# Operand steps one block ahead and W_out's parts on GpSimd's queue, in a hybrid encoder block

## The chip, the cores and the metric

The kernel runs on one core of one Trainium2 chip. The metric is the device time of one execution in microseconds. It is stated as the median of several runs; a profiled execution, taken separately, gives the trace that the views below are read from.

## What is computed

One layer on 1024 rows (tokens) of 1024 features in fp32: a SwiGLU feed-forward, a mixer (eight forgetting-attention heads beside an RG-LRU channel group) and a second feed-forward, each with a scaled residual and a layer norm:

```python
def layer_norm(x, g, b):
    mu = jnp.mean(x, axis=-1, keepdims=True)
    var = jnp.mean(jnp.square(x - mu), axis=-1, keepdims=True)
    return (x - mu) * lax.rsqrt(var + LN_EPS) * g + b

def swiglu(x, w_gate, w_up, w_down):
    return (jax.nn.silu(x @ w_gate) * (x @ w_up)) @ w_down

x = layer_norm(DN_ALPHA * x + 0.5 * swiglu(x, ffn1...), ln1_g, ln1_b)
z = x @ w_in                       # q, k, v, LRU inputs and gates, forget gates
fox = forgetting_attention(q, k, v, fg)     # softmax(q.k/8 + cum[t] - cum[s]) v, causal
lru = jax.nn.gelu(z_gate) * rg_lru(causal_conv(z_x))
x = layer_norm(DN_ALPHA * x + concat([fox, lru]) @ w_out, ln2_g, ln2_b)
x = layer_norm(DN_ALPHA * x + 0.5 * swiglu(x, ffn2...), ln3_g, ln3_b)
```

`D_MODEL` is 1024, `D_FF` 4096, the attention has 8 heads of 64 features, `cum` is the running sum of log forget gates.

## The kernel before

**Splitting.** TensorE multiplies fp32r operands. To keep fp32 accuracy each operand is split in two: ScalarE casts the high part, VectorE subtracts it from the source for the low part, and `mm3` (L159) sums three products, high by high, high by low and low by high. So nearly all the time of the kernel is 128x512 matmuls in threes, and each operand costs one ScalarE and one VectorE instruction ahead of them.

**Feed-forward.** `gate_up` (L334) computes x·W_gate and x·W_up for 16 pairs of 128 columns. Each product of a pair is done by a 2x2 block scheme with seven block products (`one` to `seven`, L650 to L672) whose operands are sums and differences of blocks, named "11", "t1", "22", "t2", "21", "t4", "t3" on the weights' side. In each pair `weights` (L361) loads 1 MB of W_gate and of W_up (SyncE's queue, L364; two buffers) and makes the seven split operands of each in a ring of 16 `ws` buffers. The first pair of the first feed-forward, `first_pair` (L376), has its ScalarE, VectorE and TensorE order written by hand, because it runs while x and the first weights still arrive. `down_ffn` (L740) is the third matrix.

**Steps done on the side.** The second feed-forward's first pair must start right behind the attention. Its seven operands of both matrices are therefore prepared during the first feed-forward by a generator, `prepare` (L263): a step loads a 128x256 block of the second W_gate or W_up into one of two `aux` buffers (L272), splits it (ScalarE L278, VectorE L279, in one buffer of the same `ws` ring), takes differences in place (L290, L296, L302, L307) and stores the two parts to a scratch tensor `pre_d` by GpSimd's queue (L285). Sixteen later steps do the same, without differences, for the attention half of W_out, into `wo_d` (L316, L317). `gate_up` calls for one step behind products `two` and `five` of each matrix of each pair from pair 1 on (L728), four in a pair; a step ends at a `yield`.

**Attention.** `attention` (L1122) goes through 64 units, one of 128 queries of one head each, heads 0 to 5 in turn from the longest unit to the shortest, then heads 6 and 7 interleaved. A unit's scores are computed by TensorE (L1158, L1159); GpSimd masks the diagonal block of `cum` in place (L1162); VectorE forms the logits from scores and `cum` with their extremum (L1164, which reads what the mask of the next shorter unit will write); ScalarE takes the exponentials (L1165). Three units later the probabilities are transposed (L1179), split (L1183, L1184) and multiplied with the values (L1200). A head's operands q, k (two parts), cum and v are loaded by SyncE's queue when the previous head reaches its third unit (`load`, L1132), two heads' buffers in all. Until unit 35, tiles of the W_out product for the LRU half fill TensorE (L1263). The attention half needs `wo_d`'s four pairs of parts (`ready_out_w`, L1114: SyncE's queue, one pair each at units 45, 47, 49, 51), in the eight `ws` buffers that the LRU half's parts had, and three of four pairs of `mix` blocks, the heads' outputs, which go out to DRAM by GpSimd's queue (L1216) and come back by SyncE's at units 40, 50, 52 (L1269). Behind the third of these stand norm 2's g and b, each broadcast to all partitions (`load_gb`, L188). They take the same eight `h` buffers, in order of asking. Output tiles with their norm (`layer_norm`, L195) follow from the last units on.

**Norm.** `layer_norm` subtracts the mean and multiplies by g (L205), then finds 1/sqrt(var + eps) from ScalarE's square root, a reciprocal and a Newton step (L206 to L210), and multiplies and adds b (L212). The Newton step here yields the negated factor, and `load_gb` negates g once by GpSimd (L192) to undo it.

**What sets the order.** A planner orders each engine's instructions at build time, by their place in the text and by when its model of the times holds them ready; on each engine, and on each engine's DMA queue, that order is then fixed, and an instruction that waits holds up what is behind it. `issue_after(x)` puts the instructions of its block that are on x's engine behind x. `fetch` (L99) keeps such a chain among SyncE's loads. `ready_pair` (L546) loads the prepared operands for the second feed-forward by SyncE's queue (L556).

Of the kernel before, what the change touches and what calls it, by code (L numbers as in the profile page):

```python
# [9 lines left out]
F32 = mybir.dt.float32  # L10
# [7 lines left out]
P = 128  # L18
# [41 lines left out]
class Block:  # L60
# [127 lines left out]
    def load_gb(self, g, b, gb):  # L188

        for t, v in zip(gb, (g, b)):  # L190
            self.fetch(t, bass.AP(tensor=v.tensor, offset=v.offset, ap=[[0, P], [1, D]]))
        self.nc.gpsimd.tensor_scalar(gb[0], gb[0], -1.0, 1.0, op0=ALU.mult, op1=ALU.mult)  # L192
        self.gb = gb

    def layer_norm(self, i, done=None):  # L195

        nc, v, gb = self.nc, self.nc.vector, self.gb
        a = self.acc[i]
        st = self.small.tile([P, 2, 6], F32, tag="st", name=self.nm("st"))
        for j in range(2):  # L200
            v.bn_stats(st[:, j, :], a[:, j * H:(j + 1) * H])
        s = self.small.tile([P, 8], F32, tag="ln", name=self.nm("ln"))
        mv, sd, y, w = s[:, 0:2], s[:, 2:3], s[:, 3:4], s[:, 4:5]
        v.bn_aggr(mv, st)
        v.scalar_tensor_tensor(a, a, mv[:, 0:1], gb[0], op0=ALU.subtract, op1=ALU.mult)  # L205
        nc.scalar.activation(sd, mv[:, 1:2], AF.Sqrt, bias=self.eps)  # L206
        v.tensor_scalar(w, mv[:, 1:2], EPS, 0.5, op0=ALU.add, op1=ALU.mult)
        v.reciprocal(y, sd)
        v.scalar_tensor_tensor(w, y, w, y, op0=ALU.mult, op1=ALU.mult)
        v.scalar_tensor_tensor(y, w, 1.5, y, op0=ALU.subtract, op1=ALU.mult)  # L210
        for ds in (slice(0, H), slice(H, D)) if done else (slice(0, D),):
            v.scalar_tensor_tensor(a[:, ds], a[:, ds], y, gb[1][:, ds], op0=ALU.mult, op1=ALU.add)  # L212
            if done:
                done(i, ds)
# [48 lines left out]
    def prepare(self, views, to_d, w_out, wsp, ap):  # L263

        nc, v = self.nc, self.nc.vector

        def raw():
            return ap.tile([P, 2, P], F32, tag="aux", name=self.nm("aux"))

        def load(view, k, c):  # L270
            t = raw()
            nc.sync.dma_start(t, view[:, k:k + 2, c * P:(c + 1) * P])  # L272
            return t

        def halves(src):
            t = wsp.tile([P, 4, P], F32R, tag="ws", name=self.nm("ws"))
            hi, lo = t[:, 0:2, :], t[:, 2:4, :]
            nc.scalar.copy(hi, src)  # L278
            v.tensor_tensor(lo, src, f32(hi), ALU.subtract)  # L279
            return t  # L280

        for m, view in enumerate(views):
            for h in range(2):
                def out(n, src):
                    nc.gpsimd.dma_start(to_d[m, OPERANDS.index(n), h], f32(halves(src)))  # L285

                up, down = 2 * h, 4 + 2 * h
                a, b = load(view, up, 0), load(view, up, 1)
                out("11", a)
                v.tensor_tensor(b, b, a, ALU.subtract)  # L290
                a = load(view, down, 1)
                yield
                out("t1", b)
                yield
                out("22", a)
                v.tensor_tensor(a, a, b, ALU.subtract)  # L296
                b = load(view, down, 0)
                yield
                out("t2", a)
                yield  # L300
                out("21", b)
                v.tensor_tensor(b, b, a, ALU.subtract)  # L302
                a = load(view, down, 1)
                yield
                out("t4", b)
                b = load(view, up, 1)
                v.tensor_tensor(a, a, b, ALU.subtract)  # L307
                yield
                out("t3", a)
                yield  # L310
        self.wo_d = self.dram.tile([FOX // P, P, 2, D], F32, name="wo_d")
        for f in range(FOX // P):
            for c in range(4):
                cols = slice(c * 2 * P, (c + 1) * 2 * P)
                a = raw()
                nc.sync.dma_start(a.rearrange("p k c -> p (k c)"), w_out[f * P:(f + 1) * P, cols])  # L316
                nc.gpsimd.dma_start(self.wo_d[f, :, :, cols], f32(halves(a)).rearrange("p (l k) c -> p l (k c)", l=2))  # L317
                yield

    def gu_views(self, *ws):  # L320
        return [w.rearrange("(k p) f -> p k f", p=P) for w in ws]
# [12 lines left out]
    def gate_up(self, wg, wu, h_d, rows, bank, tp, wsp, raws=None, later=None, aside=None, ready=None, steps=None):  # L334
# [26 lines left out]
        def weights(pair, view, w):  # L361

            r = self.raw([P, KT, 2 * P])
            nc.sync.dma_start(r, view[:, :, pair * 2 * P:(pair + 1) * 2 * P])  # L364
            b11, b12, b21, b22 = quarters(r)
            w["11"] = parts(b11)
            w["21"] = parts(b21)
            t1 = less(b12, b11)
            t2 = less(b22, t1)
            w["t2"] = parts(t2)  # L370
            w["t1"] = parts(t1)
            w["t3"] = parts(less(b22, b12))
            w["22"] = parts(b22)
            w["t4"] = parts(less(b21, t2))
# [171 lines left out]
        def ready_pair(g, u):  # L546
# [10 lines left out]
                                      ready[both.index(m), OPERANDS.index(n)].rearrange("h p (l k) f -> l p h k f", l=2)[l])  # L557
                m.w[n] = to

            for n in ("11", "21", "t1"):  # L560
                for m in both:
                    fetch(n, m, two_blocks())
            for n in ("t4", "t2"):
                r = self.rawp.tile([P, 4, 4, P], F32R, tag="raw", name=self.nm("raw"))
                for i, m in enumerate(both):
                    fetch(n, m, (r[:, 2 * i], r[:, 2 * i + 1]))
            t21 = [block() for _ in range(4)]
            g.sum, u.sum = self.sum_bank(), self.sum_bank()
            g.product("11", "11", g.sum, True)
# [112 lines left out]
        for pair in range(FF // P // 2):  # L682
# [39 lines left out]
            for m in (gate, up):  # L722
# [3 lines left out]
                for step in ("two", "six", "five", "seven", "three"):  # L726
                    getattr(m, step)()
                    if steps and step in ("two", "five"):  # L728
                        next(steps, None)

                def pending(m=m, gate=gate, g=(g0, g1), end=end, last=pair == FF // P // 2 - 1):
                    m.four()
# [381 lines left out]
    def ready_out_w(self):  # L1114

        for f in range(FOX // P):
            hl = tuple(self.wsp.tile([P, 4 * VW], F32R, tag="ws", name=self.nm("w"))[:, 0:D] for _ in range(2))
            for l in range(2):
                self.nc.sync.dma_start(f32(hl[l]), self.wo_d[f, :, l])
            yield hl  # L1120

    def attention(self, w_out, mixp, ln, normed):  # L1122
# [7 lines left out]
        with self.pool("att_p", 3) as pp, self.pool("att_t", 1) as tp, self.pool("att_pt", 6) as ptp, self.pool("att_qk", 2, side="right") as qkp:  # L1130
# [110 lines left out]
            for n in range(len(units) + AHEAD + 1):  # L1241
# [18 lines left out]
                if fill and (n < 2 or n % 8 in (2, 3, 4)):  # L1260
                    i, d = fill.pop(0)
                    with self.tc.issue_after(scores.ins) if n < 3 else nullcontext():
                        self.down_tile(i, lru_tiles, 1.0, (d,))  # L1263
                if 45 <= n < 53 and n % 2:
                    w_fox.append(next(w_steps))
                if n in MIXES:
                    mix.append(tuple(self.hp.tile([P, T], F32R, tag="h", name=self.nm("mix")) for _ in range(2)))
                    for l in range(2):
                        nc.sync.dma_start(f32(mix[-1][l]), mix_d[len(mix) - 1][l])  # L1269
                    if len(mix) == 3:  # L1270
                        self.load_gb(*ln, [self.hp.tile([P, T], F32, tag="h", name=self.nm("gb")) for _ in range(2)])
                if tiles:
                    out_tile()
            return tiles, out_tile
# [140 lines left out]
```

## Time and profile before

| | us |
|---|---|
| runs: median of 3 (lowest, highest) | 2322.07 (2321.42, 2322.68) |
| profiled execution: time | 2323.19 |
| its span, first to last instruction | 2321.5 |
| TensorE busy with matmuls | 2298.7 |
| VectorE busy | 1635.6 |
| ScalarE busy | 1019.1 |
| GpSimd busy | 227.8 |

The mean granted TensorE clock is 0.997. How to read the lines in the next sections: a row of a timeline is the start, the duration, engine, line, operation, written and read tile, and in brackets the idle time of the engine just before and what ended it; a row of waits is the waiting engine and line, what it waited for, total us, times and the longest; SPq and POOLq are the DMA issues of SyncE's and GpSimd's queues. Matmuls are pipelined: a 128x512 one is listed with 0.39 us while the next starts 0.23 us behind it.

### The profile page before, as it was taken

The page shows a single profiled execution, that of the slowest core. Times are in us where ns is not written, and L with a number is a line of the kernel's source. Part 1 is how long each engine was busy: PE and PEld are TensorE (multiplying, and loading weights), DVE is VectorE, ACT ScalarE, POOL GpSimd, SP SyncE. Part 2 cuts the span into 40 slices and gives each one's busy share as a digit, 9 for nine tenths or more (in the row PEclk, how much of TensorE's full clock was granted, in tenths as well). Part 3 has the DMA queues.
Part 4 walks back from the last instruction along what each step waited for, and adds up shares of the span by engine and source line. Part 5 has one row for each costly group of instructions (what it writes and reads, how often), then busy time and mean ns, then how long its engine had stood idle before and what let it go on. Part 6 is the DMA issues. An engine that isn't in the chain of part 4 may idle for free.

```text
span 2321.5 us, 28560 instructions
## 1 busy us (share of the span) xinstructions
PE 2298.7 (99%) x10705; PEld 1914.1 (82%) x10705; DVE 1635.6 (70%) x2521; ACT 1019.1 (44%) x1623; POOL 227.8 (10%) x388
## 2 busy tenths in 40 slices
PE   8999999999999999999999999999999999999998
PEld 7888888888888888888898788888888888888887
DVE  7867666666467788866667899565656665577886
ACT  5443434343344345453556755334333333344341
POOL 0121111100000000111133210000000000000000
PEclk9999999999999999999999999999999999999999
DMA  4444444433276433233274934232323232564542
GB/s 150 141 141 145 139 147 141 146 113 125 101 259 234 147 127 109 75 92 110 91 218 126 283 137 141 86 118 89 122 93 123 87 118 87 195 244 168 182 144 73
DMA packets 194444, 323.08 MB, mean 139 GB/s; under 512 B 10033, under 2 KB 115825, under 8 KB 194305
## 3 DMA queue, kind: packets, MB, share of 16 engines
q1 hardware_dynamic: 167712, 230.74, 30.9%
q0 software_dynamic: 26592, 90.51, 9.9%
q8 instruction: 84, 1.38, 0.3%
q14 instruction: 56, 0.45, 0.1%
HBM read 226.81 MB, written 94.40 MB: 138 GB/s over the span
## 4 chain that ended last, share of the span: by engine, by line
PE 81%; issue 10%; DVE 3%; DMA 3%; POOL 2%; ACT 1%; SPq 0%; POOLq 0%; DVEq 0%; ACTq 0%
PE x L163 7%; PE x L164 7%; PE x L165 7%; PE s L165 6%; PE s L164 6%; PE s L163 6%; PE a L165 6%; PE a L164 6%; PE a L163 6%; PE b L163 6%; PE b L164 6%; PE b L165 6%; PE a L1200 1%; PE a L1179 1%; PE a L1049 1%
## 5 line engine op out<-in xcount | busy, mean ns | idle before, releaser
L349 ACT CAST ws<-t 128x512 fp32r<-128x512 f32 x240 | 148.9, 623 | 374.2 <-PE b L164 253.0
L349 ACT CAST ws<-raw 128x512 fp32r<-128x512 f32 x180 | 111.0, 622 | 239.3 <-PE x L164 237.3
L350 DVE TENSOR_TENSOR ws<-t,ws 128x512 fp32r<-128x512 f32 x240 | 164.3, 686 | 56.4 <-ACT ws L349 50.6
L350 DVE TENSOR_TENSOR ws<-raw,ws 128x512 fp32r<-128x512 f32 x180 | 123.3, 688 | 114.4 <-ACT ws L349 110.3
L164 PE MATMUL a<-ws,ws 128*128 128x512 f32 x512 | 199.8, 390 | 0.2
L163 PE MATMUL a<-ws,ws 128*128 128x512 f32 x512 | 199.3, 390 | 0.4 <-ACT row L672 0.4
L163 PE MATMUL b<-As,ws 128*128 128x512 f32 x512 | 199.4, 389 | 0.2 <-ACT row L663 0.2
L164 PE MATMUL b<-As,ws 128*128 128x512 f32 x512 | 199.3, 389 | 0.0
L165 PE MATMUL b<-As,ws 128*128 128x512 f32 x512 | 199.2, 389 | 0.0
L165 PE MATMUL a<-ws,ws 128*128 128x512 f32 x512 | 199.2, 389 | 0.0
L163 PE MATMUL x<-As,ws 128*128 128x512 f32 x504 | 196.6, 390 | 2.1 <-ACT row L659 2.0
L164 PE MATMUL x<-As,ws 128*128 128x512 f32 x504 | 196.1, 389 | 0.0
L165 PE MATMUL x<-As,ws 128*128 128x512 f32 x504 | 196.1, 389 | 0.0
L163 PE MATMUL x<-A,ws 128*128 128x512 f32 x496 | 193.3, 390 | 0.0
L165 PE MATMUL x<-A,ws 128*128 128x512 f32 x496 | 193.0, 389 | 0.0
L164 PE MATMUL x<-A,ws 128*128 128x512 f32 x496 | 193.0, 389 | 0.0
L772 ACT CAST ws<-raw 128x1024 fp32r<-128x1024 f32 x112 | 117.4, 1050 | 157.8 <-PE a L164 87.2
L775 DVE TENSOR_TENSOR ws<-raw,ws 128x1024 fp32r<-128x1024 f32 x112 | 136.6, 1220 | 53.0 <-ACT ws L772 52.6
L702 POOL DMA_DIRECT2D h_d<-row x96 | 68.9, 719 | 968.5 <-DVE row L696 928.4
L163 PE MATMUL s<-ws,ws 128*128 128x512 f32 x384 | 149.5, 389 | 0.0
L165 PE MATMUL s<-ws,ws 128*128 128x512 f32 x384 | 149.4, 389 | 0.0
L164 PE MATMUL s<-ws,ws 128*128 128x512 f32 x384 | 149.4, 389 | 0.0
(295 smaller groups left out, 5252.7 us busy)
## 6 DMA issues: line engine op xcount, KB each, us to landing
raw<-h_d SPq DMA_DIRECT2D x56, 1024.0 KB, 5.4
h_d<-row POOLq DMA_DIRECT2D x96, 512.0 KB, 3.5
wd<-in_ffn_w_down_dram SPq DMA_DIRECT2D x32, 1024.0 KB, 7.5
raw<-in_ffn_w_gate_dram SPq DMA_DIRECT2D x30, 1024.0 KB, 5.3
raw<-in_ffn_w_up_dram SPq DMA_DIRECT2D x30, 1024.0 KB, 5.3
h_d<-row POOLq DMA_DIRECT2D x32, 256.0 KB, 2.7
raw<-in_w_in_dram SPq DMA_DIRECT2D x16, 512.0 KB, 4.9
pre_d<-ws POOLq DMA_DIRECT2D x28, 256.0 KB, 2.7
```

What stands on the lines that cost most here:

```text
L163: mm(out, ah, bh, start=first, stop=False, skip_group_check=goes_on)
L164: mm(out, ah, bl, start=False, stop=False, skip_group_check=goes_on)
L165: mm(out, al, bh, start=False, stop=last, skip_group_check=goes_on)
L349: nc.scalar.copy(hi, src)
L350: v.tensor_tensor(lo, src, f32(hi), ALU.subtract)
L702: nc.gpsimd.dma_start(d[:, 2 * n:2 * n + 2], t.rearrange("p (r t) -> p r t", r=2))
L772: cast = nc.scalar.copy(hi, src)
L775: self.mark = v.tensor_tensor(lo, src, f32(hi), ALU.subtract)
L1049: nc.tensor.matmul(pa[:, 0:width], xh, wh[:, 0:width], start=k == 0, stop=False)
L1179: nc.tensor.transpose(pa[:, (j % 4) * P:(j % 4 + 1) * P], p[:, j * P:(j + 1) * P], self.ident)
L1200: mm(pv[:, ps], vt[:, j, :], pts[h, qt][j // 4][l][:, j % 4, ps], start=j == 0 and l == 0, stop=j == last and l == 1)
```

## The change

Four things. In `prepare`, each block is loaded one step ahead of the step that uses it, so the order within the steps is shifted by one `yield`; W_out's steps too. 45 steps result where there were 44. In `gate_up`, the steps' SyncE instructions are put behind the pair's load of W_up. In the attention, W_out's parts are loaded by GpSimd's queue, at units 37, 39, 41 and 43, norm 2's vectors at unit 38 instead of with the third mix block at 52, and `ready_pair`'s first loads are put behind the last mix load. In the norms, g stays as it is, and the Newton step gives the factor with its own sign.

```diff
         for t, v in zip(gb, (g, b)):
             self.fetch(t, bass.AP(tensor=v.tensor, offset=v.offset, ap=[[0, P], [1, D]]))
-        self.nc.gpsimd.tensor_scalar(gb[0], gb[0], -1.0, 1.0, op0=ALU.mult, op1=ALU.mult)
...
-        v.tensor_scalar(w, mv[:, 1:2], EPS, 0.5, op0=ALU.add, op1=ALU.mult)
+        v.tensor_scalar(w, mv[:, 1:2], EPS, -0.5, op0=ALU.add, op1=ALU.mult)
...
-        v.scalar_tensor_tensor(y, w, 1.5, y, op0=ALU.subtract, op1=ALU.mult)
+        v.scalar_tensor_tensor(y, w, 1.5, y, op0=ALU.add, op1=ALU.mult)
...
                 up, down = 2 * h, 4 + 2 * h
                 a, b = load(view, up, 0), load(view, up, 1)
-                out("11", a)
-                v.tensor_tensor(b, b, a, ALU.subtract)
+                yield
+                keep(m, h, "11", a)
+                less(b, a)
                 a = load(view, down, 1)
                 yield
-                out("t1", b)
+                keep(m, h, "t1", b)
                 yield
-                out("22", a)
-                v.tensor_tensor(a, a, b, ALU.subtract)
+                keep(m, h, "22", a)
+                less(a, b)
                 b = load(view, down, 0)
...
-                out("t4", b)
+                keep(m, h, "t4", b)
                 b = load(view, up, 1)
-                v.tensor_tensor(a, a, b, ALU.subtract)
                 yield
-                out("t3", a)
-                yield
+                less(a, b)
+                keep(m, h, "t3", a)
...
                 nc.sync.dma_start(a.rearrange("p k c -> p (k c)"), w_out[f * P:(f + 1) * P, cols])
+                yield
                 nc.gpsimd.dma_start(self.wo_d[f, :, :, cols], f32(halves(a)).rearrange("p (l k) c -> p l (k c)", l=2))
-                yield
...
-            nc.sync.dma_start(r, view[:, :, pair * 2 * P:(pair + 1) * 2 * P])
+            self.weight_load = nc.sync.dma_start(r, view[:, :, pair * 2 * P:(pair + 1) * 2 * P])
...
+            with self.tc.issue_after(self.mix_load.ins):
+                for n in ("11", "21", "t1"):
+                    for m in both:
+                        fetch(n, m, two_blocks())
...
                     if steps and step in ("two", "five"):
-                        next(steps, None)
+                        with self.tc.issue_after(self.weight_load.ins):
+                            next(steps, None)
...
-                self.nc.sync.dma_start(f32(hl[l]), self.wo_d[f, :, l])
+                self.nc.gpsimd.dma_start(f32(hl[l]), self.wo_d[f, :, l])
...
-                if 45 <= n < 53 and n % 2:
+                if 36 <= n < 44 and n % 2:
                     w_fox.append(next(w_steps))
+                if n == 38:
+                    self.load_gb(*ln, [self.hp.tile([P, T], F32, tag="h", name=self.nm("gb")) for _ in range(2)])
                 if n in MIXES:
...
-                        nc.sync.dma_start(f32(mix[-1][l]), mix_d[len(mix) - 1][l])
-                    if len(mix) == 3:
-                        self.load_gb(*ln, [self.hp.tile([P, T], F32, tag="h", name=self.nm("gb")) for _ in range(2)])
+                        self.mix_load = nc.sync.dma_start(f32(mix[-1][l]), mix_d[len(mix) - 1][l])
```

More of the change, by code (lines that the diff above doesn't have):

```diff
@@ L280, in halves, with keep, less @@
             return t
+        def keep(m, h, n, src):
+            nc.gpsimd.dma_start(to_d[m, OPERANDS.index(n), h], f32(halves(src)))
+        def less(x, y):
+            v.tensor_tensor(x, x, y, ALU.subtract)
+        self.wo_d = self.dram.tile([FOX // P, P, 2, D], F32, name="wo_d")
         for m, view in enumerate(views):
             for h in range(2):
-                def out(n, src):
-                    nc.gpsimd.dma_start(to_d[m, OPERANDS.index(n), h], f32(halves(src)))
                 up, down = 2 * h, 4 + 2 * h
                 a, b = load(view, up, 0), load(view, up, 1)
-                out("11", a)
-                v.tensor_tensor(b, b, a, ALU.subtract)
+                yield
+                keep(m, h, "11", a)
+                less(b, a)
                 a = load(view, down, 1)
                 yield
-                out("t1", b)
+                keep(m, h, "t1", b)
                 yield
-                out("22", a)
-                v.tensor_tensor(a, a, b, ALU.subtract)
+                keep(m, h, "22", a)
+                less(a, b)
                 b = load(view, down, 0)
                 yield
-                out("t2", a)
+                keep(m, h, "t2", a)
                 yield
-                out("21", b)
-                v.tensor_tensor(b, b, a, ALU.subtract)
+                keep(m, h, "21", b)
+                less(b, a)
                 a = load(view, down, 1)
                 yield
-                out("t4", b)
+                keep(m, h, "t4", b)
                 b = load(view, up, 1)
-                v.tensor_tensor(a, a, b, ALU.subtract)
                 yield
-                out("t3", a)
-                yield
-        self.wo_d = self.dram.tile([FOX // P, P, 2, D], F32, name="wo_d")
+                less(a, b)
+                keep(m, h, "t3", a)
         for f in range(FOX // P):
@@ L558, in fetch @@
                 m.w[n] = to
[L560 to L566, printed above, removed]
+            with self.tc.issue_after(self.mix_load.ins):
+                for n in ("11", "21", "t1"):
+                    for m in both:
+                        fetch(n, m, two_blocks())
+                for n in ("t4", "t2"):
+                    r = self.rawp.tile([P, 4, 4, P], F32R, tag="raw", name=self.nm("raw"))
+                    for i, m in enumerate(both):
+                        fetch(n, m, (r[:, 2 * i], r[:, 2 * i + 1]))
             t21 = [block() for _ in range(4)]
```

## The prediction

> **What bounds the kernel now.** I read the page first, then TensorE's waits, then the chain of waits and the timelines at the few places where TensorE waits at all.
>
> ```profile
> span 2321.5 us, 28560 instructions
> PE 2298.7 (99%) x10705; PEld 1914.1 (82%) x10705; DVE 1635.6 (70%) x2521; ACT 1019.1 (44%) x1623; POOL 227.8 (10%) x388
> PE b L163 <- ACT ws L443: 2.8, 1, 2.8
> PE s L1158 <- DVE m L1164: 2.4, 7, 0.9
> PE x L163 <- ACT row L659: 2.0, 3, 1.2
> PE a L165 <- DMA mix<-mix_d: 0.2, 1, 0.2
> ```
>
> TensorE is busy for 2298.7 of 2321.5 us, and the change touches none of its 10705 matmuls. What can be won is therefore idle time, 22.8 us in all, and the part near the edits is the four rows above (total, times, longest), 7.4 us. 0.2% of the time, about what a measurement of this kernel can tell from no change, is 4.6 us. What can be lost is not bounded in this way: any new wait of TensorE counts in full.
>
> **The change, part by part.**
>
> *The prepared steps.* In the kernel before, the first step loads two blocks and at once subtracts them (L290) ahead of its first yield. The planner put that subtraction far ahead of its place in the text. Chain of waits and the engines' timelines, first 51 us (start, duration, and in brackets the idle time before and what ended it):
>
> ```profile
> 11.03 8.45 DMA aux<-in_ffn_w_gate_dram
> 17.73 3.66 PE L249 MATMUL b<-ident,x 128*128 128x128 f32 x32
> 50.30 0.39 SPq L364 DMA_DIRECT2D raw<-in_ffn_w_up_dram  x1
> 15.62 1.29 DVE L391 TENSOR_TENSOR ws<-raw,ws 128x512 fp32r<-128x512 f32 x2
> 19.57 0.43 DVE L290 TENSOR_TENSOR aux<-aux,aux 128x256 f32<-128x256 f32 x1 [2.66 <-DMA aux<-in_ffn_w_gate_dram]
> 19.91 0.68 DVE L391 TENSOR_TENSOR ws<-t,ws 128x512 fp32r<-128x512 f32 x1
> 23.56 0.58 ACT L443 COPY ws<-b 128x512 f32<-128x512 f32 x1
> 24.19 0.50 PE L163 MATMUL b<-A,ws 128*128 128x512 f32 x1 [2.80 <-ACT ws L443]
> ```
>
> VectorE finished at 15.62 + 1.29 = 16.91 and then stood 2.66 us before an operation that belongs to the second feed-forward layer, because that one's block landed as the last of the start-up loads. What first_pair needed next (L391) began at 19.91 instead of 16.91: 3.0 us late. ScalarE's copy at 23.56 comes behind it, and with it TensorE's 2.80 us. After the change the subtraction stands behind a yield, and the two loads are issued behind pair 1's load of w_up, which in the old trace goes out at 50.30 us; the subtraction cannot start before that. So the 3.0 us on VectorE go. What is late next? The transposes feeding that copy end at 17.73 + 3.66 = 21.39, so TensorE can go on there instead of at 24.19: 2.8 us.
>
> The stall has a second part. Stretches of 1 us: length, busy of TensorE, weight load, VectorE, ScalarE and GpSimd, granted clock, DMA share, GB/s:
>
> ```profile
> 25.00:26.00 1.00, 1.00 (x5) 0.84 (x4) 1.00 (x2) 0.66 (x2) 0.00 (x0) 0.80 0.00 0
> 26.00:27.00 1.00, 1.00 (x4) 0.72 (x4) 0.91 (x3) 0.79 (x2) 0.00 (x0) 0.50 0.00 0
> 27.00:28.00 1.00, 1.00 (x4) 0.81 (x3) 1.00 (x2) 1.00 (x3) 0.00 (x0) 0.50 0.00 0
> 28.00:29.00 1.00, 1.00 (x4) 0.81 (x3) 0.65 (x2) 0.78 (x2) 0.00 (x0) 0.50 0.00 0
> ```
>
> The granted clock fell to 0.50 for about 3.4 us right behind the wait (0.80 is 0.4 us at half clock, then 3 us whole). Half of 3.4 is 1.7 us of matmul time lost, and I expect no such dip when the wait is gone. The Trainium skill, "TensorE: Matmul & The Clock Gate", Part 1, states that the clock halves after at least one idle window of about 3.4 us. Here 2.8 us of idling did it, so the measurement goes by a looser rule than the page's; strictly by the page the dip would have another cause, and could stay, which leaves 2.8 us instead of 4.5.
>
> Together 4.5 us at most. But VectorE sets a second limit later in the same pair:
>
> ```profile
> 28.51 0.69 DVE L436 TENSOR_TENSOR row<-b,row 128x512 f32<-128x512 f32 x1 [0.35 <-PE b L165]
> 31.56 0.69 DVE L436 TENSOR_TENSOR row<-b,row 128x512 f32<-128x512 f32 x1 [0.56 <-PE b L165]
> 56.97 0.68 DVE L391 TENSOR_TENSOR As<-ws,As 128x512 fp32r<-128x512 f32 x1
> 57.71 0.50 PE L164 MATMUL b<-As,ws 128*128 128x512 f32 x1
> ```
>
> The matmul at 57.71 reads the low part that VectorE ended at 57.65: no slack there. TensorE can be ahead at that point only by what VectorE is ahead: 3.0 us, plus what its own waits for TensorE give back (0.35 and 0.56, 0.9 in all). I take **3.6 us** between 3.0 and 3.9 (2.8 and 4.5 as outer bounds).
>
> In the other pairs the steps run in bunches behind the pair's splits. Where ScalarE stood before a DMA, TensorE's three L659 waits came right after:
>
> ```profile
> 168.17 0.41 ACT L278 CAST ws<-aux 128x256 fp32r<-128x256 f32 x1 [0.70 <-DMA aux<-in_ffn_w_gate_dram]
> 398.87 0.62 ACT L349 CAST ws<-t 128x512 fp32r<-128x512 f32 x1 [2.19 <-DMA wo_d<-ws]
> 437.83 0.62 ACT L349 CAST ws<-t 128x512 fp32r<-128x512 f32 x1 [2.38 <-DMA wo_d<-ws]
> ```
>
> The first waited for a block; this is what loading a step ahead removes. The other two waited for a split buffer still being stored to W_out's scratch, and the change leaves these stores, two to four of them in a bunch, as they are. The number of casts and subtractions is unchanged (the subtractions move a step; one more step is needed, 45 for 44). Of the 2.0 us in the row of waits I take **0.8 us** as gained. It can be 2.0 (all three go) or a loss: with the phase shifted by one step another bunch may be hit, at most again 1.2 as the longest. SyncE's extra order, steps behind weight loads, costs nothing: no ScalarE or VectorE wait of size there is for a weight block.
>
> *The attention.* W_out's eight loads go from SyncE's queue, at units 45 to 51, to GpSimd's, at 37 to 43; norm 2's two vectors go from the last place on SyncE's queue to unit 38; the negation (L192) goes. What moves in the DMA engines (issues with KB each and median us to landing; then stretches of 4 us as above):
>
> ```profile
> w<-wo_d SPq DMA_DIRECT2D x8, 512.0 KB, 10.3
> mix_d<-mix POOLq DMA_DIRECT2D x6, 512.0 KB, 8.3
> gb<-in_ln_g_dram SPq DMA_DIRECT2D x1, 512.0 KB, 6.7
> 1284.00:1288.00 4.00, 4.00 (x25) 3.44 (x24) 3.33 (x7) 2.60 (x7) 0.29 (x1) 1.00 0.10 29
> 1288.00:1292.00 4.00, 4.00 (x31) 3.67 (x29) 2.69 (x6) 1.92 (x5) 1.40 (x3) 1.00 1.00 329
> 1304.00:1308.00 4.00, 3.72 (x29) 3.16 (x28) 3.78 (x10) 3.49 (x10) 0.52 (x2) 1.00 1.01 244
> 1332.00:1336.00 4.00, 4.00 (x33) 3.77 (x31) 4.00 (x10) 2.83 (x6) 0.58 (x2) 1.00 0.94 336
> ```
>
> From 1288 to 1336 us the DMA engines are full (share 1.01, 1.00, 0.94). The change puts two W_out parts (2 MB) and the vectors (1 MB) from the end of this stretch to its beginning, in front of or beside the operands of heads 6 and 7. Those are what ends waits there:
>
> ```profile
> 1298.93 9.90 DMA cum<-cum_d
> 1309.19 0.30 POOL cum L1162
> 1310.01 0.50 PE s L1158
> 1333.40 4.76 DMA mix<-mix_d
> 1288.64 1.11 POOL L1216 DMA_DIRECT2D mix_d<-mix  x2 [2.02 <-ACT mix L1212]
> 1293.33 0.29 POOL L1162 TENSOR_SCALAR_AFFINE_SELECT cum<-cum 128x128 f32<-128x128 f32 x1 [2.44 <-DVE m L1164]
> 1340.59 1.05 POOL L192 TENSOR_SCALAR gb<-gb 128x1024 f32<-128x1024 f32 x1 [2.23 <-DMA gb<-in_ln_g_dram]
> 1345.09 1.27 DVE L205 SCALAR_TENSOR_TENSOR row<-row,ln,gb 128x1024 f32<-128x1024 f32 x1
> ```
>
> Head 6's sums of gates (cum) took 9.90 us to land; GpSimd's mask (L1162) waited for them, then VectorE, then TensorE at 1310.01. What delays such a load delays TensorE one for one, less what VectorE and TensorE have in hand. Bounds: 3 MB in front of these operands take 9 us at 336 and 12 at 244 GB/s, the worst case. Below nothing: two of W_out's parts no longer stand ahead of head operands on SyncE's own queue, and TensorE's seven waits for L1164 (2.4 us) could shrink. While the heads' half-height blocks ran alone the engines moved 244 GB/s, against 329 and 336 beside other transfers, so part of the moved 3 MB fits into what is full only by share. I take a loss of **1.5 us**, near the lower end because of these rows. At the end of the stretch the third mix block (landed 1333.40 + 4.76, TensorE's 0.2 us row) comes earlier, as nothing but the second mix is still ahead of its store: **0.2 us** gained, or **0.3** with what VectorE takes from it.
>
> GpSimd's eight issues: two took 1.11 us for mix_d, blocks of the same 512 KB, so 4.4 us in all, 1.1 at a time. Queued behind them is L1162, the mask, for which VectorE's L1164 waits. Their cover are GpSimd's gaps (2.44 us in the row shown, ended by VectorE): cost nothing; 4.4 us if they fell outside. Their own wait, for the buffers of W_out's other half, ends with the last of the filling tiles, ahead of unit 36. Norm 2's vectors land in about 7 us; from unit 38 on that is long before L205 at 1345.09, which even in the old order began 3.4 us behind the negation (1340.59 + 1.05). So negation and vectors are worth nothing, and in norms 1 and 3, where the vectors are loaded two products ahead of the first norm, nothing too. The signs in the norm cost no instruction. The first blocks of ready_pair come behind the last mix load; SyncE then waits for the attention's memory anyway, and TensorE needs them only after the attention: nothing, or at worst about the 8.3 us that a transfer of this stage took (the mix_d row).
>
> **The sum.** Start -3.6, bunches -0.8, attention +1.5 - 0.3 = +1.2: **-3.2 us**. The profiled execution took 2323.19 us (1.7 of it outside the span), so 2320.0; the median of the runs, 2322.07, lies 1.1 lower: **2318.9 us**, 0.14% down.
>
> **The rivals.** *All of it is won.* Start 4.5, L659's waits 2.0, and 1.2 in the attention (the mix wait and half of the L1164 row): -7.7, or 2314.4 us. For it: one planner error and its echo in the clock, and loads with less ahead of them on their own queue. Against: VectorE has no slack at 57.7 us, and two of the three L659 waits come from stores that stay.
>
> *The planner puts another step there.* The change moves the subtraction but doesn't fix its place; if a load or an operation of the steps again stands in first_pair's way, the start gains nothing, and what is left is -0.8 + 1.2: 2322.5 us, no change. For it: the planner did it once. Against: the loads now have a fixed place behind the pair 1 load at 50.3 us.
>
> *Slower: the last heads' operands come late.* Full DMA engines from 1288 us on, with W_out's 4 MB served beside SyncE's queue, deliver heads 6 and 7 up to the 12 us later that the 3 MB take at 244 GB/s. It decides from 9.0 us, since 4.4 are won before. At 10 us it gives 2322.1 - 4.4 + 10 = 2327.7 us. For it: share 1.0 throughout, and GpSimd's in-order mask already waits for cum. Against: a fuller DMA mix moved 329 and more GB/s. The Trainium skill, "DMA: Bandwidth & Descriptors", section Issuing engines are not separate DMA queues, says that all queues run on the same 16 engines and interleave, so that another issuing engine saves issue time only. The rows agree: by that rule GpSimd's queue adds no capacity, and it is the rule that speaks against this edit.
>
> **How the numbers follow.** Forecast (2317.0 with 3.9 at the start, 1.2 in the bunches and an even attention, to 2321.0 with 3.0, 0.4 and 2.3 lost): 0.50. All won: 0.27. Another step there: 0.13. Slower: 0.10. Of the forecast's cases 0.03 lie under 2317.4 (more than 4.6 us down): faster 0.30; slower 0.10; same 0.60. The range reaches down to all won, 2314.0, and up beyond the case without the start's gain, 2325.0; outside lie the slower case and the tail of the best.
>
> **What would show it.** In the first 25 us no L290 ahead of L391, TensorE at the copy's matmul by about 21.4 us instead of 24.19, and no clock of 0.50 behind it; TensorE's "b L163 <- ACT ws L443" row gone. At 57.7 us the same matmul some 3.6 us earlier. L659's total near 1.2. W_out's loads on GpSimd from about 1288 us, L1162 not later for them, cum of heads 6 and 7 landing 0 to 3 us later in their stage, the mix wait gone. Wrong it would be if TensorE's waits between 1300 and 1340 grew by more than 3 us, or if L443's wait stayed.

## The result and the profile after

| | before | after |
|---|---|---|
| runs: median (lowest, highest), us | 2322.14 (2321.42, 2322.68) | 2329.99 (2328.75, 2331.68) |
| profiled execution, us | 2323.19 | 2329.6 |

Six runs of each give a ratio of 1.0035, 95% interval 1.0023 to 1.0047: the change costs 7.9 us, where 3.2 us were forecast as a gain. The forecast's range ended at 2325.0.

The page of the kernel after, its span and TensorE's busy time:

```profile
span 2327.9 us, 28563 instructions
PE 2299.1 (99%) x10705; PEld 1914.3 (82%) x10705; DVE 1634.9 (70%) x2521; ACT 1019.0 (44%) x1623; POOL 228.3 (10%) x393
```

The same matmuls, and 28.8 us beside them where there were 22.8. TensorE's waits (total, times, longest) say which idle time went and which came. The line numbers have moved by 3 or 4 (L1164 is L1168, L1158 is L1162, L659 is L662):

```profile
PE s L1162 <- DVE m L1168: 9.9, 7, 7.6
PE b L248 <- DMA row<-in_x_dram: 2.5, 4, 1.1
PE s L1162 <- DMA kh<-k_d: 1.5, 1, 1.5
PE x L163 <- ACT row L662: 1.0, 2, 0.5
```

The L443 row (2.8) and the mix row (0.2) are gone and L662 has halved. The scores' wait for VectorE has grown from 2.4 to 9.9 us, by one wait of 7.6, and a wait for the DMA of `kh` is new.

**The start** came out as forecast. Timeline of the kernel after, TensorE, SyncE and VectorE, and two stretches of 1 us, columns as in the prediction:

```profile
18.01 3.66 PE L248 MATMUL b<-ident,x 128*128 128x128 f32 x32
21.81 0.50 PE L163 MATMUL b<-A,ws 128*128 128x512 f32 x1
...
46.30 0.40 SPq L366 DMA_DIRECT2D raw<-in_ffn_w_up_dram  x1
46.75 2.40 SPq L271 DMA_DIRECT2D aux<-in_ffn_w_gate_dram  x2
...
53.71 0.50 PE L164 MATMUL b<-As,ws 128*128 128x512 f32 x1
...
58.38 0.42 DVE L285 TENSOR_TENSOR aux<-aux,aux 128x256 f32<-128x256 f32 x1
```

```profile
26.00:27.00 1.00, 1.00 (x6) 0.84 (x5) 1.00 (x3) 0.40 (x1) 0.00 (x0) 1.00 0.00 0
27.00:28.00 1.00, 1.00 (x6) 0.84 (x5) 1.00 (x2) 0.00 (x0) 0.00 (x0) 1.00 0.00 0
```

The first subtraction has gone from 19.57 to 58.38 us, TensorE goes on at 21.81 instead of 24.19, the clock stays at 1.00 where it was 0.50, and the matmul of 57.71 us is at 53.71.

**The attention** is where the time was lost. GpSimd's timeline, then the chain of waits, both of the kernel after:

```profile
1301.80 0.29 POOL L1166 TENSOR_SCALAR_AFFINE_SELECT cum<-cum 128x128 f32<-128x128 f32 x1 [0.20 <-DVE m L1168]
1311.67 0.54 POOL L1166 TENSOR_SCALAR_AFFINE_SELECT cum<-cum 128x128 f32<-128x128 f32 x2 [9.58 <-DMA cum<-cum_d]
```

```profile
1289.23 10.24 DMA kh<-k_d
...
1299.53 7.14 SPq L1275
...
1306.76 2.28 SPq L1275
...
1313.02 13.11 DMA kh<-k_d
...
1326.27 1.19 PE s L1162 x2
```

GpSimd stood 9.58 us before head 6's mask, because that head's `cum` had not landed. But the chain does not go through this wait. It goes through SyncE's queue: the loads of mix block 1 (L1275) stand in it, the first takes 7.14 us to issue, and head 7's `kh` behind them lands at 1313.02 + 13.11 = 1326.13 us. TensorE's first score of head 7 starts at 1326.27. In the kernel before that score started at 1320.16 us. Issue of head 5's v and of head 7's second `kh` block and that score, first of before, then the two issues of after:

```profile
1286.42 0.37 SPq L1144 DMA_DIRECT2D v<-v_d  x1
1311.90 0.59 SPq L1140 DMA_DIRECT2D kh<-k_d  x1
1320.16 0.47 PE L1158 MATMUL s<-kh,q 128*128 128x512 f32 x1
```

```profile
1281.41 0.37 SPq L1148 DMA_DIRECT2D v<-v_d  x1
1313.02 0.59 SPq L1144 DMA_DIRECT2D kh<-k_d  x1
```

Counted from the issue of head 5's v, `kh` lands 11.1 us later than before (44.7 against 33.6). Of these 6.1 are a later issue (31.6 against 25.5 us behind v) and 5.0 a longer transfer (13.1 against 8.1).

So the kernel after, 4.0 us ahead at the start's end, is 6.1 us behind at this score, and 6.4 behind at the end of the span. Issues with KB and median time to landing from 1281 to 1330 us, first of before, then of after:

```profile
kh<-k_d SPq DMA_DIRECT2D x4, 256.0 KB, 7.7
cum<-cum_d SPq DMA_DIRECT2D x2, 512.0 KB, 9.7
```

```profile
w<-wo_d POOLq DMA_DIRECT2D x8, 512.0 KB, 18.6
mix<-mix_d SPq DMA_DIRECT2D x4, 512.0 KB, 13.4
kh<-k_d SPq DMA_DIRECT2D x4, 256.0 KB, 12.5
cum<-cum_d SPq DMA_DIRECT2D x2, 512.0 KB, 14.1
```

The heads' loads take 4.4 to 4.8 us longer, W_out's 8.3 (10.3 before). And the engines meanwhile (2 us stretches of after):

```profile
1306.00:1308.00 2.00, 0.00 (x0) 0.00 (x0) 0.00 (x0) 0.00 (x0) 0.00 (x0) 1.00 1.05 293
1308.00:1310.00 2.00, 0.00 (x0) 0.00 (x0) 0.00 (x0) 0.00 (x0) 0.00 (x0) 0.72 1.01 398
...
1312.00:1314.00 2.00, 1.28 (x4) 1.08 (x5) 1.76 (x8) 1.24 (x4) 1.09 (x4) 0.50 1.05 381
1314.00:1316.00 2.00, 2.00 (x10) 1.81 (x10) 0.87 (x4) 0.60 (x3) 0.47 (x1) 0.57 1.08 414
```

TensorE stands still while the DMA engines are full (share 1.05 and 1.01), and when it goes on the clock is at half. A second dip stands behind the wait for `kh`:

```profile
1324.00:1328.00 4.00, 2.54 (x11) 1.57 (x11) 3.22 (x7) 3.16 (x8) 1.38 (x5) 0.74 0.98 251
1328.00:1332.00 4.00, 4.00 (x27) 3.66 (x26) 1.12 (x2) 1.12 (x3) 1.33 (x3) 0.83 0.70 279
```

Means of 0.74 and 0.83 over 4 us are 3.4 us at half clock in all, nearly all of it behind the score at 1326.27: about 1.5 us lost there, an estimate from these two rows.

### The profile page after: what moved, and what is told of

The parts are those of the page before. It is cut to its first block, busy times and chain, and to the rows that moved or that the text cites. A ratio compares the mean times of both kernels' runs of the same rounds, so it can differ in the third digit from the quotient of the medians.

```text
span 2327.9 us, 28563 instructions
## 1 busy us (share of the span) xinstructions
PE 2299.1 (99%) x10705; PEld 1914.3 (82%) x10705; DVE 1634.9 (70%) x2521; ACT 1019.0 (44%) x1623; POOL 228.3 (10%) x393
## 4 chain that ended last, share of the span: by engine, by line
PE 85%; issue 7%; DVE 3%; DMA 2%; POOL 1%; ACT 1%; SPq 1%; DVEq 0%; POOLq 0%; ACTq 0%
PE x L163 8%; PE x L164 8%; PE x L165 8%; PE b L163 6%; PE b L164 6%; PE b L165 6%; PE s L165 6%; PE s L164 6%; PE s L163 6%; PE a L163 6%; PE a L165 6%; PE a L164 6%; PE a L1204 1%; DMA kh<-k_d 1%; PE a L1183 1%
```

## The experiments

**Theory A:** the start's gain is real, and the loss is the attention's alone: W_out's loads on GpSimd's queue share the full DMA engines with the operands of heads 6 and 7, which come late. Its rivals: the new step order costs later (B); the early units are the fault, on whichever queue (C); the vectors or the held operands (D); GpSimd's own order (E, later J against A2). Each ratio is taken against runs of the kernel before on the same chip; their medians were 2322.3 us (e1 to e4), 2322.5 (e6 to e9), 2322.9 (e10, e11) and 2321.8 (e12 to e14).

### Which part: e1_steps_only and e2_attention_only

```diff
# after -> e1
-            with self.tc.issue_after(self.mix_load.ins):
+            with nullcontext():
...
-                self.nc.gpsimd.dma_start(f32(hl[l]), self.wo_d[f, :, l])
+                self.nc.sync.dma_start(f32(hl[l]), self.wo_d[f, :, l])
-                if 36 <= n < 44 and n % 2:
+                if 45 <= n < 53 and n % 2:
...
-                if n == 38:
-                    self.load_gb(*ln, [self.hp.tile([P, T], F32, tag="h", name=self.nm("gb")) for _ in range(2)])
...
+                    if len(mix) == 3:
+                        self.load_gb(*ln, [self.hp.tile([P, T], F32, tag="h", name=self.nm("gb")) for _ in range(2)])
```

The second is the reverse: these lines put into the kernel before, and nothing else.

> The kernel after, with its attention edits taken back: W_out's parts on SyncE's queue at units 45 to 51, norm 2's vectors behind the last mix load, the down pass's kept operands tied to nothing; the new step order and the sign of the norm stay. Theory A (the loss is all in the attention, because W_out's 4 MB on GpSimd's queue share the DMA engines with head 6's operands; the start's gain is real): the wait of 7.81 us at 1304.8 us is gone, the start's 21.4 us wait stays at 0.3 us; 2317.5 us, 2316 to 2319. Rival B (the new step order itself costs time later, and the attention only shows it): still slower than before, 2324 to 2330 us.

> The kernel before with the attention edits alone: W_out's parts on GpSimd's queue at units 37 to 43, norm 2's vectors at 38, the down pass's kept operands behind the last mix load; steps and the norm's sign as before. Theory A: the attention's loss comes alone, with the start's 2.8 us wait still there: 2333.5 us, 2331 to 2336, a TensorE wait of 6 to 9 us near 1309 us. Rival B (the loss needs the new step order): 2320 to 2324 us, and no such wait.

Measured: steps and norm alone 2317.53 us (2315.99 to 2320.3), ratio 0.998, interval 0.9972 to 0.9989, 4.8 us faster than before and 12.5 faster than the kernel after. The attention's edits alone 2332.34 us (2331.72 to 2333.39), ratio 1.0044, 1.0031 to 1.0058, 10.1 us slower. Both as theory A has it, and B falls. Chain of waits of the attention alone:

```profile
1299.61 17.51 DMA cum<-cum_d
...
1317.48 0.41 POOL gate_raw L1189
...
1323.20 8.35 DMA kh<-k_d
...
1331.68 0.47 PE s L1159
```

Here it is the copy of the sums' ratios (`gate_raw`) that stands behind head 6's mask on GpSimd, and TensorE waits 8.9 us for it; again head 7's `kh` comes after that, at 1331.55.

### What won the start: e9_start_only and e10_pin_only

```diff
# before -> e9
                 a, b = load(view, up, 0), load(view, up, 1)
+                yield
                 out("11", a)
...
                 out("t3", a)
-                yield
# before -> e10
-            nc.sync.dma_start(r, view[:, :, pair * 2 * P:(pair + 1) * 2 * P])
+            self.weight_load = nc.sync.dma_start(r, view[:, :, pair * 2 * P:(pair + 1) * 2 * P])
...
-                        next(steps, None)
+                        with self.tc.issue_after(self.weight_load.ins):
+                            next(steps, None)
```

> The kernel before with one line moved: the last pause of each half's steps stands behind the first two loads of a half instead of at its end, so the first subtraction no longer waits on a load at the start. The bunches, the attention and the norm's sign are as before. Theory A (of the 4.75 us that steps and norm won in an earlier run, the start is the most, by its wait of 2.8 us and 3.4 us at half clock): the wait at 21 us is under 0.5 us, 2318.5 us, 2317 to 2320. Rival F (the order of the steps over the whole pass wins it, or the norm's sign): the start's wait goes, but the time is 2320.5 to 2322.5 us.

> The kernel before with the steps' instructions queued behind the last weight load, and nothing else of the change: the steps keep their old order with the load and its subtraction in one step. The earlier run that moved the pause alone kept the start's wait of 2 us, since the first loads still went out at 10.8 us. Theory A (the start is won by the tie to the weight load, which holds the first loads back until 46 to 50 us, and by nothing else): no L443 wait, the start's idle time 4 us lower as in the run with steps and norm alone, bunches as before: 2318.5 us, 2317 to 2320. Rival G (the pause is needed as well, since the subtraction now waits in VectorE's order for a load that comes at 54 us): a wait of over 2 us near 55 us in place of the one at 24 us, 2320.5 to 2323 us.

The pause alone: 2321.24 us (2320.47 to 2323.75), ratio 0.9996, 0.9987 to 1.0005, no change that can be told. The tie alone: 2319.25 us (2317.85 to 2320.61), ratio 0.9984, 0.9975 to 0.9993, 3.7 us won. TensorE's wait for the start's copy in the one and the other:

```profile
PE b L163 <- ACT ws L443: 2.0, 1, 2.0
```

```profile
PE b L163 <- ACT ws L443: 0.2, 1, 0.2
```

A pause moves a step in the text, but the planner pulls it forward again: the run with the pause still issues the first two blocks at 10.78 us and has the subtraction at 20.29. The tie to the weight load holds the loads until 47.09 us, and the subtraction follows at 58.72. Rival G falls too: no wait took its place.

### Queue or place: e3_w_on_sync, e4_w_late, e6_gb_early, e7_w_held

```diff
# after -> e3
-                self.nc.gpsimd.dma_start(f32(hl[l]), self.wo_d[f, :, l])
+                self.nc.sync.dma_start(f32(hl[l]), self.wo_d[f, :, l])
# after -> e4
-                if 36 <= n < 44 and n % 2:
+                if 45 <= n < 53 and n % 2:
# after -> e6: both of these
# after -> e7 (self.mask is the latest unit's mask)
-            for l in range(2):
-                self.nc.gpsimd.dma_start(f32(hl[l]), self.wo_d[f, :, l])
+            with self.tc.issue_after(self.mask.ins):
+                for l in range(2):
+                    self.nc.gpsimd.dma_start(f32(hl[l]), self.wo_d[f, :, l])
-                if 36 <= n < 44 and n % 2:
+                if 52 <= n < 56:
```

> The kernel after with one word changed: W_out's parts load by SyncE's queue, at the same units 37 to 43. Theory A (it is the second queue, whose transfers run beside head 6's): the early loads now stand in the one queue, some of them ahead of head 6's operands, so head 6 is late by their transfer time only, about 1.25 us for each of some 4 parts or pairs ahead of it: wait of 0 to 4 us, 2318 to 2323 us. Rival C (it is the early place, whichever queue): a wait as long as after's, 2328 to 2332 us.

> The kernel after with one number pair changed: W_out's parts load by GpSimd's queue, but at units 45 to 51, where before has them. Theory A (the place of a load on GpSimd's queue is set by when its buffer comes free, since nothing else on that queue holds it back, and not by the unit): no change, 2330 us, 2328 to 2332, the wait of 7 to 9 us near 1305 us stays. Rival C (the early units are the fault): the loads come behind head 6's, the wait is under 2 us, 2318 to 2322 us.

> The kernel after with W_out's parts back on SyncE's queue at units 45 to 51; norm 2's vectors stay at unit 38, the down pass's kept operands behind the last mix load. It splits the earlier run with W_out's parts on SyncE's queue at units 37 to 43 (2324.2 us) from the one with all attention edits undone (2317.5 us). Theory A (what costs is the bytes that stand ahead of or beside head 6's operands: W_out's 4 MB or the 3 MB of it ahead, while the vectors are 1 MB): 2318 us, 2317 to 2320, head 6's forgetting sums some 2 us later than with all undone. Rival D (the vectors at unit 38 or the held operands are half of the loss): 2321 to 2324 us.

> The kernel after, W_out's parts still on GpSimd's queue, but at units 52 to 55 and each behind the mask of that unit on GpSimd, so that none is issued before head 7's forgetting sums have landed. Theory A (GpSimd's queue does harm only by when it issues): head 6's operands land some 5 us sooner than in the kernel after, no TensorE wait over 3 us, 2320 us, 2317.5 to 2323 (norm 2's vectors and mix 1 still stand ahead of heads 6 and 7 in SyncE's queue). Rival E (the issue work of eight loads on GpSimd, or the masks' order on it, is what stalls): the wait of 7 us or more stays, 2328 to 2332 us.

Late units on GpSimd's queue: 2330.56 us (2328.64 to 2331.17), ratio 1.0035, 1.0022 to 1.0049, the kernel after over again. The planner issues such a load as soon as its buffer is free, from 1281 us on; the unit in the text holds nothing. C falls in this form. But on SyncE's queue at the early units the time is 2324.17 us (2321.66 to 2325.98), ratio 1.0007, 0.9998 to 1.0016: 5.8 us better than after and still 6.6 worse than with all undone, above theory A's 2318 to 2323. So the second queue is not all of it. With W_out's parts late on SyncE's queue and the vectors early: 2318.24 us (2315.93 to 2320.0), ratio 0.998, 0.9971 to 0.999; vectors and held operands cost next to nothing, and D falls. With W_out's loads alone put back, then, the whole loss is gone.

Held back on GpSimd's queue behind head 7's masks: 2324.28 us (2322.93 to 2326.25), ratio 1.0008, 0.9999 to 1.0017, outside what theory A gave (2317.5 to 2323), though head 6's operands are in time again. Waits of TensorE and a later stretch of this run:

```profile
PE a L164 <- DMA w<-wo_d: 2.2, 2, 1.4
PE s L1163 <- DVE m L1169: 2.1, 6, 0.9
```

```profile
1330.00:1340.00 10.00, 6.93 (x19) 4.44 (x18) 3.13 (x8) 1.16 (x4) 0.58 (x2) 0.66 1.05 403
```

The heads' wait is down to what before had, on the same queue as in after. Now W_out's parts themselves are late, and the granted clock is 0.66 behind these waits.

### Bytes or order: e11_half_w, e8_cum_first, e12_masks_in_order, e14_masks_ratio, e13_steps_masks

```diff
# after -> e11
-            for l in range(2):
-                self.nc.gpsimd.dma_start(f32(hl[l]), self.wo_d[f, :, l])
-            yield hl
+            self.nc.gpsimd.dma_start(f32(hl[0]), self.wo_d[f, :, 0])
+            yield hl[0], hl[0]
# after -> e8: the load of cum moved ahead of the loads of q, kh, kl in load(h)
# after -> e12 (and e1 -> e13)
-                nc.gpsimd.affine_select(cum[:, ts], ...)
+                with self.tc.issue_after(self.mask.ins) if self.mask else nullcontext():
+                    self.mask = nc.gpsimd.affine_select(cum[:, ts], ...)
# e12 -> e14
-                    nc.gpsimd.tensor_copy(self.gate_raw.rearrange(...), ...)
+                    nc.scalar.copy(self.gate_raw.rearrange(...), ...)
```

> The kernel after, but only the high half of each of W_out's parts is loaded, four loads of 512 KB instead of eight, and stands in for the low half too; the low half's values are left out. Everything else, the order on both queues too, stays. Theory A (head 6's operands are late by the bytes that the engines move beside them: W_out's loads and the operands take turns): with 2 MB instead of 4 MB beside them the sums of head 6 land 2.5 to 4 us sooner than the 17.3 us in the kernel after, the wait of 7.8 us falls to 3 to 5 us: 2325 us, 2322 to 2327.5. Rival H (it is the second queue as such, not the bytes; or norm 2's vectors and mix 1, which stay): 17 us to land and the wait of over 7 us stay, 2329 to 2332 us.

> The kernel after, but every head's forgetting sums are issued first of its loads instead of behind its q and k parts. Theory A (the engines are shared: head 6's k parts land at 1306 to 1309 us as well, so the tile of unit 48 is late with or without its mask): a wait of 4 to 7 us stays, 2327 us, 2325 to 2330. Rival E (only GpSimd's order stalls: the masks of units 46 and 47 stand behind that of unit 48, which waits for the sums alone): the wait falls under 2 us, 2318 to 2322 us.

Half of W_out's bytes, the low half's values left out: 2326.04 us (2324.94 to 2327.49), ratio 1.0014, 1.0004 to 1.0023, 4.0 us better than after, within A's range; H falls. The longest wait, though, only fell to 6.3 us, and head 6's `cum` still took 15.91 us: the two MB that are left are the first two, and these stand beside head 6's operands. `cum` first: 2334.52 us (2333.12 to 2338.89), ratio 1.0055, 1.0041 to 1.0068. E said 2318 to 2322 and falls; A's 2325 to 2330 is passed as well: head 7's last `kh` now lands 49.0 us behind head 5's v, 44.7 in after.

With W_out's parts on SyncE's queue `cum` of head 6 had landed as late (1311.2 us), yet GpSimd had only this idle time before its mask, since head 5's masks stood ahead of it:

```profile
1311.25 0.29 POOL L1166 TENSOR_SCALAR_AFFINE_SELECT cum<-cum 128x128 f32<-128x128 f32 x1 [2.29 <-DMA cum<-cum_d]
```

From this came theory A2: part of the loss is GpSimd's order.

> The kernel after, with every mask of the attention (the triangle that GpSimd lays on a head's forgetting sums) queued behind the mask before it, so that head 6's first mask no longer stands ahead of head 5's last two; the loads keep their order on both queues. Theory A2 (the loss has two parts: the sums of head 6 land some 8 us later, and GpSimd, which waits for them in order, holds back head 5's last tiles too; with W_out's parts on SyncE's queue the sums landed as late, but the masks stood in the other order, and 6 us less were lost): the masks of head 5 are out before the sums land at 1311 us, TensorE's longest wait falls to 2 to 5 us: 2326 us, 2323.5 to 2328.5; one ratio copy of head 5 still stands behind head 6's mask and may keep a wait of its own. Rival J (order on GpSimd means nothing, the late operands alone cost): 2329 to 2332 us, a wait of 7 us or more.

> The kernel after, with the masks in order as in the run beside it, and the copy of the sums' ratios, which TensorE's transpose waits for, on ScalarE instead of GpSimd; the loads keep their order. Nothing that TensorE needs for head 5 then stands behind head 6's mask. Theory A2: the late landing alone is left, as in the run with W_out's parts on SyncE's queue: 2324 us, 2322 to 2326.5, longest wait 1 to 3 us. Rival J (the late operands alone cost): 2329 to 2332 us.

> The kernel with all attention edits undone (steps and the norm's sign kept, 2317.5 us in its run), and the masks in order on GpSimd. There GpSimd waits 2.28 us for head 6's sums with two masks of head 5 behind it, and TensorE's waits for VectorE behind those masks are 2.1 us in seven places. Theory A2: 0 to 1.5 us are won: 2316.5 us, 2315.5 to 2318. Rival J: no change, 2317 to 2318 us; slower if the fixed order hinders another tile.

Measured: masks in order 2330.69 us (2329.32 to 2331.92), ratio 1.0037, 1.0024 to 1.005; with the ratio copy on ScalarE 2331.05 us (2328.83 to 2332.29), ratio 1.0038, 1.0025 to 1.0051. Nothing is won: A2 falls, and J's times hold. The run with the masks in order shows why. Its waits, then its chain:

```profile
PE s L1162 <- DMA kh<-k_d: 9.2, 2, 6.6
PE s L1162 <- DVE m L1169: 2.2, 6, 0.9
```

```profile
1298.43 7.10 SPq L1277
...
1311.84 13.09 DMA kh<-k_d
1324.94 0.14 issue
1325.07 0.77 PE s L1162
```

The long wait for VectorE, 7.6 us, is gone, as A2 wanted. TensorE did head 5's work earlier and then stood 6.6 us before head 7's `kh`. The order on GpSimd only chose where to wait.

In the fastest version the same order gives 2317.11 us (2315.89 to 2320.35, one run of 3292.56 aside), ratio 0.998, 0.9971 to 0.9989: no different from 2317.53.

### What all runs have in common

The last thing to arrive is head 7's second `kh` block. From the trace of each run: the loads of W_out, mix and norm 2 (in MB of 1024 KB) issued behind head 5's v that land ahead of that block; the time from the issue of head 5's v to its landing; how long after it the first score of head 7 starts; the median of the runs.

| run | MB ahead | kh lands after | score behind it | median, us |
|---|---|---|---|---|
| before | 3 | 33.6 | 0.2 | 2322.1 |
| steps only | 3 | 33.0 | 0.4 | 2317.5 |
| W_out held | 3 | 33.1 | 0.5 | 2324.3 |
| vectors early | 4 | 35.2 | 2.1 | 2318.2 |
| half of W_out | 5 | 40.8 | 1.9 | 2326.0 |
| W_out on SyncE | 6 | 43.3 | 0.1 | 2324.2 |
| after | 7 | 44.7 | 0.1 | 2330.0 |
| late units | 7 | 45.4 | 0.1 | 2330.6 |
| masks in order | 7 | 44.6 | 0.1 | 2330.7 |
| attention only | 7 | 45.0 | 0.1 | 2332.3 |
| masks and ratio copy | 7 | 46.2 | 0.1 | 2331.1 |
| `cum` first | 7 | 49.0 | 0.1 | 2334.5 |
| pause alone | 3 | 33.5 | 0.2 | 2321.2 |
| tie alone | 3 | 33.5 | 0.1 | 2319.3 |
| steps, masks in order | 3 | 33.3 | 0.1 | 2317.1 |

The landing goes with the MB ahead, 11 to 13 us for 4 MB, whether these go by one queue or two. The run with `cum` first lies above this (49.0 us); there head 7's `cum`, half a MB, stands ahead of `kh` as well, which does not explain all of it. In before the first score began 0.2 us behind the landing, so there was little to spare. Measured against the steps alone, 10 to 13 us more cost 6.6 us (W_out on SyncE) to 13.5 us (masks and ratio copy). Two rows stand apart. With the vectors early and with half of W_out the score came about 2 us behind the landing, so `kh` was not its last limit; with half of W_out TensorE's wait of 6.3 us behind head 6's mask came before it. And the time of W_out held was lost behind that score.

The rest of the program, from that score on, takes about the same in before (2321.5 - 1320.16 = 1001.3 us) and after (2327.9 - 1326.27 = 1001.6). Over all runs it is 998.4 to 1003.1 us, and 1007.8 with W_out held.

Two things stay open. W_out on SyncE's queue, with 6 MB ahead, is 1.8 us faster than half of W_out with 5. In the traces its first score comes no sooner, but the rest is 2.7 us shorter (998.4 against 1001.1), and its mean granted clock from 1300 to 1340 us is 1.00 against 0.91; which of this decides was not taken apart. And how much of the loss is the half clock was not measured by itself; the 1.5 us worked out above is an estimate.

## Why the prediction was wrong

- *What bounds the kernel.* Right: the matmuls are untouched, and any new wait counts in full.
- *The start, -3.6.* Right in size: the tie alone won 3.7 us (interval 1.6 to 5.8), the clock's dip went with the wait, and the matmul of 57.71 us came 4.0 earlier, about the upper end (3.9) of what VectorE allowed. Of the two reasons given only one holds: the loads' place behind the weight load, not the yield.
- *The bunches, -0.8.* Not shown by itself: L659's 2.0 us are 1.0 after and 1.3 with the steps alone, but over the runs with the new steps this row goes from 0.4 to 1.8. Steps and norm without the attention won 4.8 us, against 4.4 worked out.
- *Norm, vectors' place, ready_pair, GpSimd's issue time: nothing.* Right for the vectors and `ready_pair`: with the one early and the other held the time is 2318.24 us, 0.7 from that without. GpSimd's eight issues did not delay the heads where they came late (waits for VectorE of 2.1 us with W_out held). The norm's sign was never run alone.
- *The attention, +1.5 - 0.3 = +1.2.* **This step failed.** It costs 10.1 us alone and 12.5 beside the steps. Head 6's `cum` took 17.3 us to land (9.9 before), where 0 to 3 us more were expected, and TensorE's waits between 1300 and 1340 us grew from 3.3 to 12.0 us, where 3 more were named as the sign of being wrong. The worst case (9 to 12 us for 3 MB) covers the 11.1 us by which head 7's `kh` came later, but partly by luck: 4 MB more stood ahead, at 2.8 us each instead of 3 to 4. The value was taken near the lower end, since "part of the moved 3 MB fits into what is full only by share". The whole stretch, of before and of after, shows how much fitted:

```profile
1284.00:1326.00 42.00, 40.12 (x272) 34.20 (x270) 34.37 (x85) 31.11 (x78) 11.40 (x29) 1.00 0.94 277
```

```profile
1284.00:1326.00 42.00, 31.33 (x209) 26.40 (x207) 27.75 (x71) 25.65 (x65) 12.36 (x31) 0.92 1.03 317
```

The engines did move more, 317 instead of 277 GB/s, 1.7 MB in 42 us; but 4 MB more stood ahead, for the prediction missed that mix block 1 too would go in front of head 7. The Trainium skill, "DMA: Bandwidth & Descriptors", section Queues, rings and completion order, says that each engine goes round robin between the queues that have work for it; the rows agree, as W_out's loads by GpSimd take 18.6 us (10.3 before) and `kh` beside them 12.5 (7.7). With all of them on SyncE's queue `kh` landed nearly as late (43.3 us against 44.7), so taking turns is not the main part of that delay. The prediction had the neighbouring rule of that page as the one that speaks against this edit, and gave it too little weight.
- *W_out's loads go out from about 1288 us.* Wrong: from 1282 us, and the units in the text, which the prediction reasoned with, do not hold them (2330.56 us at the late units).
- *The rival "Slower: the last heads' operands come late"* is what happened. Its sum was 2322.1 - 4.4 + the delay. With head 7's delay of 44.7 - 33.6 = 11.1 us it gives 2328.8; measured were 2329.99. Its chance of 0.10 was too low: that share 1.0 throughout leaves nothing to give was in the rows quoted, and the argument against it (329 GB/s and more) came from stretches in which other blocks moved. "The planner puts another step there" did not happen: the start's gain came.

## What to carry to other kernels

Where the DMA share is 1.0 ahead of a deadline, count the bytes that are queued in front of the last operand, over all queues; what was moved there in this case delayed it by 11 to 13 us for 4 MB, and another queue did not help. Where an instruction must not go early, tie it to one on its own engine, since a later place in the text holds nothing back. And when the longest wait is taken away, look which arrival is next: here a wait of 7.6 us went and one of 6.6 took its place.

## What the runs showed of the hardware

One issue itself was held up: behind head 6's loads, most of them still under way, the issue of one mix load on SyncE took 7.14 us, where those of the kernel before took 0.32 to 0.48, and all loads behind it went out later. In no trace did SyncE issue a load before the load eight places ahead of it had landed. Where the DMA engines are full this holds up the queue too: in the kernel after the issue of `cum` at 1294.26 us follows such a landing at 1294.19, and that of `kl` at 1315.99 one at 1315.97. Whether the program or the chip sets the eight is not shown.

The clock: 2.0 us of waiting at the start (the pause alone) left it at 1.00, 2.8 us (before) brought 0.50. But 1.5 us before head 7's `kh` (after) were followed by half clock too, and so were waits of 0.4 and 1.4 us within 2.3 us in the run with W_out held (0.50 from 1333 us on). The length of a wait alone therefore does not decide. The Trainium skill, "TensorE: Matmul & The Clock Gate", Part 1, has a free-running window of about 3.4 us. The long wait of after fits it: TensorE stopped at about 1305 us, the clock fell in 1308 to 1310. The short waits show that a single gap of that length is not needed.
